# First norm of a hybrid diffusion layer: scale and shift made by blocks of channels, tokens scaled before they are transposed

## The chip, the cores and the metric

The kernel runs on one core of a Trainium2 chip, as one program. The metric is the device time of one execution in microseconds (us). Three executions of the kernel before were timed, and one more was profiled; every duration below is from that profiled one.

## The reference

One trunk layer: a modulated RMSNorm, a token mixer (latent attention beside a bidirectional mLSTM) and a mixture of 16 experts, all in float32. The change touches the first norm and what feeds it:

```python
mod_l = silu(c) @ w_mod + b_mod              # latent tokens
mod_c = silu(c_ctx) @ w_mod + b_mod          # context tokens
sh1, sc1, ... = split(mod_l, 6)              # each 1024 channels
h_l = rmsnorm(x, norm1) * (1 + sc1) + sh1    # x:   1024 tokens x 1024 channels
h_c = rmsnorm(ctx, norm1) * (1 + sc1c) + sh1c  # ctx: 256 tokens x 1024
z = h @ w_in                                 # 1024 x 4864, the input projection
```

## The kernel before

Tokens are worked in three segments of 512, 512 and 256 (the last is the context). For each segment the norm's result is wanted with channels on partitions: `hT` holds, for each of the 8 blocks `d` of 128 channels, the value rounded to fp32r (`hT[0]`) and the rest (`hT[1]`). A projection block `b` (128 of the output columns) then takes 8 x 3 matmuls: for every `d`, high weight times `hT[0]`, high weight times `hT[1]`, low weight times `hT[0]`. ScalarE makes the high weight `whi` from the loaded `wraw`, VectorE the low one `wlo`.

Scale and shift of the first norm, each 1024 channels for two kinds of token, come from two 1024 x 1024 weights, loaded in 16 tiles `wm` of 512 KB.

- Scale (`scale(k)`, L265): TensorE, with two columns of silu(c) as the stationary operand and 512 weights moving, twice per tile `k`. A tile is one block of inputs, so all eight are needed before any channel is done; the sum `mps` is copied, turned by 8 small transposes (L290) and finished in `a1`.
- Shift (`shift(k)`, L258): VectorE, one multiply with a sum along the row for each tile and each kind of token (L263). A tile is one block of outputs. The result is `b1`.
- Tokens: ScalarE squares each tile `x` (128 tokens) and sums (`jkx`, L237), VectorE makes the reciprocal root (`rstd_dve`), then four matrices `dg`, the identity times a token's factor. `turn_x` multiplies `x` by `dg`, which turns and scales in one matmul. For segment 0 the result is copied into `xT` (L279) while scale and shift are made.
- `hidden(si, d, src)` makes `hT` of one block: ScalarE `hx` = scale times value plus shift (L300), then `hT[0]` by ScalarE for odd `d` (L302) or VectorE for even `d` (L304), then VectorE the rest (L305).

`proj` (L200) is the projection, `to_xm` copies the first `N_XM` = 3 blocks' results out. All loads are issued by SyncE in one queue. The order on each engine is not the order of the code: the tile layer sets it when the program is built, and each engine then goes through its list in that order and waits at each row for what the row needs.

Of the kernel before, what the change touches and what calls it, by code (L numbers as in the profile page):

```python
# [23 lines left out]
F32 = mybir.dt.float32  # L24
F32R = mybir.dt.float32r
BF16 = mybir.dt.bfloat16
I32 = mybir.dt.int32
AF = mybir.ActivationFunctionType
ALU = mybir.AluOpType
# [4 lines left out]
P = 128  # L34
D = 1024
# [8 lines left out]
SEGS = [(0, 512), (512, 512), (1024, 256)]  # L44
# [9 lines left out]
    _o += _w  # L54
NCOL = _o
BIG = -1.0e30
N_XM = 3
U_, WK_, KEEP_, FL_, WI_ = 3, 8, 9, 10, 11

# [15 lines left out]
def body(tc, A, out, dbg=None, upto=99):  # L75
    nc = tc.nc
    dbg = dbg or {}
    V, S, G, TE = nc.vector, nc.scalar, nc.gpsimd, nc.tensor
# [5 lines left out]
    def mm(o, l, r, start, stop):  # L84
        return TE.matmul(o, l, r, start=start, stop=stop, skip_group_check=True)  # L85
# [38 lines left out]
    def col(name, j=0, w=1):  # L124
        return cols[:, COL[name] + j:COL[name] + j + w]
# [62 lines left out]
    def fetch_w(b):  # L188
        raw[b] = pw.tile([P, 8, P], F32, name="wraw", bufs=2)
        nc.sync.dma_start(raw[b], A["win"][b])  # L190

    def split_w(b):
        if b not in raw:
            fetch_w(b)
        pool, n = (px, N_XM - 2) if 2 <= b < N_XM else (pw, 2)
        hi = pool.tile([P, 8, P], F32R, name="whi", bufs=n)
        lo = pool.tile([P, 8, P], F32R, name="wlo", bufs=n)
        split(hi, lo, raw.pop(b))
        whi[b], wlo[b] = hi, lo
# [13 lines left out]
    pm = pm_.__enter__()  # L213
    ps0_ = tc.tile_pool(name="ps0", bufs=1, space=PSUM, reuse_waits="tile")
    ps0 = ps0_.__enter__()
    xT = scratch[:, 0:4, :].rearrange("p a (b n) -> p (a b) n", n=512)
    sbc = [scratch[:, 4 + c, :] for c in range(2)]
    mrow = scratch[:2, 6, :]
    xs, diag, raw, xm = {}, {}, {}, {}

    def load_x(i):
        xs[i] = (pm if i < 4 else p0).tile([P, D], F32, name=f"x{i}")
        src = A["x"][i * P:(i + 1) * P] if i < 8 else A["ctx"][(i - 8) * P:(i - 7) * P]
        nc.sync.dma_start(xs[i], src)

    def turn_x(si, d, dst):

        for c, dg in enumerate(diag[si]):
            mm(dst[:, c * P:(c + 1) * P], xs[SEGS[si][0] // P + c][:, d * P:(d + 1) * P], dg, True, True)

    def norms(si):
        o, n = SEGS[si]
        tiles = range(o // P, (o + n) // P)
        ss = p0.tile([P, len(tiles)], F32, name=f"ss{len(tiles)}", bufs=2)
        for c, i in enumerate(tiles):
            jk = p0.tile([P, D], BF16, name="jkx", bufs=1)
            S.activation(jk, xs[i], AF.Square, accum_out=ss[:, c:c + 1])  # L237
        rstd_dve(p0, ss, ss, D)
        diag[si] = []
        for c, i in enumerate(tiles):  # L240
            dg = p0.tile([P, P], F32, name="dg", bufs=5)
            V.tensor_scalar(dg, ident, ss[:, c:c + 1], None, op0=ALU.mult)
            diag[si].append(dg)

    for i in range(4):
        load_x(i)
    for c in range(2):
        for q in range(2):
            tp = ps0.tile([P, 512], F32, name="tp", bufs=2)
            for k in range(4):  # L250
                TE.transpose(tp[:, k * P:(k + 1) * P], sil[:, 4 * q + k, c:c + 1].to_broadcast([P, P]), ident)
            S.copy(sbc[c][:, q * 512:(q + 1) * 512], tp)
    norms(0)


    mps = [ps0.tile([2, 512], F32, name="mps", bufs=2) for n in range(2)]

    def shift(k):  # L258
        wt = pm.tile([P, D], F32, name="wm", bufs=9)
        nc.sync.dma_start(wt, A["wmod_s"][k * P:(k + 1) * P])  # L260
        for c in range(2):
            jk = p0.tile([P, D], BF16, name="jk", bufs=1)
            V.scalar_tensor_tensor(jk, wt, 1.0, sbc[c], op0=ALU.mult, op1=ALU.mult, accum_out=b1[:, k, c:c + 1])  # L263

    def scale(k):  # L265
        wm = pm.tile([P, D], F32, name="wm", bufs=9)
        nc.sync.dma_start(wm, A["wmod_a"][k])
        for n in range(2):
            done = mm(mps[n], sil[:, k, :], wm[:, n * 512:(n + 1) * 512], k == 0, k == 7)
        return done  # L270

    fetch_w(0)
    for k in range(8):
        done = scale(k)
        shift(k)
        with tc.issue_after(done.ins):
            tp = ps0.tile([P, 512], F32, name="tp", bufs=2)
            turn_x(0, k, tp)
        S.copy(xT[:, k, :], tp)  # L279
    split_w(0)  # L280
    for i in range(4, 8):
        load_x(i)
    fetch_w(1)
    load_x(8)
    load_x(9)
    for n in range(2):
        S.copy(mrow[:, n * 512:(n + 1) * 512], mps[n])
    mt = ps0.tile([P, 8, 2], F32, name="mps", bufs=2)
    for j in range(8):
        TE.transpose(mt[:, j, :], mrow[:, j * P:(j + 1) * P], ident[:2, :2])  # L290
    V.tensor_tensor(a1, mt, col("bmod", 8, 8)[:, :, None].to_broadcast([P, 8, 2]), op=ALU.add)
    V.scalar_tensor_tensor(a1, a1, 1.0, col("norm1", 0, 8)[:, :, None].to_broadcast([P, 8, 2]),
                           op0=ALU.add, op1=ALU.mult)
    V.tensor_tensor(b1, b1, col("bmod", 0, 8)[:, :, None].to_broadcast([P, 8, 2]), op=ALU.add)

    def hidden(si, d, src):
        n, kind = SEGS[si][1], 0 if si < 2 else 1
# [7 lines left out]
        V.tensor_sub(hT[1][si][:, d, :], hx[:, :n], hT[0][si][:, d, :])  # L305

    for d in range(8):
        hidden(0, d, xT[:, d, :])
    pm_.__exit__(None, None, None)
    hp2 = tc.tile_pool(name="hT2", bufs=1, reuse_waits="tile")  # L310
    hpool = hp2.__enter__()
# [19 lines left out]
    for si in range(3):  # L331
        if si > 0:
            norms(si)
            for d in range(8):
                tp = ps0.tile([P, 512], F32, name="tp", bufs=2)
                turn_x(si, d, tp)
                hidden(si, d, tp[:, :SEGS[si][1]])
        for b in range(N_XM):
            to_xm(b, si)
# [632 lines left out]
class Merge:  # L972
# [11 lines left out]
    def mm(self, o, l, r, start, stop):  # L984
        return self.nc.tensor.matmul(o, l, r, start=start, stop=stop, skip_group_check=True)  # L985
# [1021 lines left out]
def arrange(inp):  # L2007

    f = {k: np.asarray(v) for k, v in inp.items()}
    ca = np.ascontiguousarray  # L2010
    A = {"x": f["x"][0], "ctx": f["ctx"][0]}
    cc = np.stack([f["c"][0], f["c_ctx"]], -1)
    A["cT"] = ca(cc.reshape(8, P, 2).transpose(1, 0, 2))
    wm = f["w_mod"][0]
    A["wmod_a"] = ca(wm[:, 1024:2048]).reshape(8, P, D)
    A["wmod_s"] = ca(wm[:, :1024].T)
    A["wmod_b"] = ca(wm[:, 2048:].T)

    def bycol(v):
        return v.reshape(-1, P).T  # L2020

    cw = f["conv_w"][0].reshape(5, 8, P).transpose(2, 1, 0).reshape(P, 40)
    A["cols"] = ca(np.concatenate([bycol(f["norm1"][0]), bycol(f["norm2"][0]), bycol(f["conv_b"][0]),
                                   bycol(f["ml_norm"][0]), bycol(f["ml_skip"][0]), bycol(f["q_norm"][0]),
                                   bycol(f["kv_norm"][0]), bycol(f["b_mod"][0]), cw], 1))
    w = f["w_in"][0]
    q, kv, kr, xm, z, ga, gb = np.split(w, np.cumsum([384, 256, 64, 1024, 1024, 1024]), axis=1)
    wp = np.concatenate([xm, q, kv, kr, kr, z, ga, gb], 1)
    A["win"] = ca(wp.reshape(8, P, 38, P).transpose(2, 1, 0, 3))
    A["wgate"] = ca(f["w_gate"][0].reshape(24, P, 16).transpose(1, 0, 2))  # L2030
    A["bgate"] = f["b_gate"][0]

    def bd(n):
        b = f[n][0].reshape(8, 32, 4, 4)
        o = np.zeros((8, 32, 4, 32, 4), b.dtype)
        i = np.arange(32)
        o[:, i, :, i, :] = b.transpose(1, 0, 2, 3)
        return o.reshape(8, P, P)

    wq = f["w_uq"][0].reshape(3, P, HEADS, 192)  # L2040
    A["wuq_n"] = ca(wq[..., :128].transpose(1, 2, 0, 3))
    A["wuq_p"] = ca(wq[..., 128:].reshape(3, P, 512).transpose(1, 0, 2))
    wk = f["w_ukv"][0].reshape(2, P, HEADS, 256)
    A["wukv_k"] = ca(wk[..., :128].transpose(2, 1, 0, 3))
    A["wukv_v"] = ca(wk[..., 128:].reshape(2, P, 4, 256).transpose(2, 1, 0, 3))
    A["wout"] = f["w_out"][0]
    A["wrouter"] = ca(f["w_router"][0].reshape(8, P, NE).transpose(1, 0, 2))
    A["final_norm"] = f["final_norm"]
    gu = np.stack([f["w_e_gate"][0], f["w_e_up"][0]], 0).reshape(2, NE, 8, P, 2, 512)

    A["wgu"] = ca(gu.transpose(1, 4, 2, 3, 0, 5).reshape(NE, 2, 4, 2, P, D).transpose(0, 1, 2, 4, 3, 5))
    A["wd"] = ca(f["w_e_down"][0].reshape(NE, 4, 2, P, D).transpose(0, 1, 3, 2, 4))
    bq, bk, bv = bd("w_qblk"), bd("w_kblk"), bd("w_vblk")
    A["bdv"] = ca(bv.transpose(1, 0, 2))
    A["bdT"] = ca(np.stack([bq, bk, bv], 1).transpose(0, 3, 1, 2))
    return A
# [17 lines left out]
```

## Time and profile before

| | us |
|---|---|
| median of 3 executions | 1984.59 |
| lowest, highest | 1984.45, 1988.88 |
| profiled execution | 1984.47 |
| its span, first to last instruction | 1982.7 |
| TensorE busy | 1906.8 (96%) |
| VectorE busy | 1375.1 (69%) |
| ScalarE busy | 1049.2 (53%) |
| mean granted TensorE clock | 0.989 of full speed |

The work is pipelined, so a busy TensorE is not one at its peak. The stage that changes lies in the first 100 us of the span.

### The profile page before, as it was taken

The page shows a single profiled execution, that of the slowest core. Times are in us where ns is not written, and L with a number is a line of the kernel's source. Part 1 is how long each engine was busy: PE and PEld are TensorE (multiplying, and loading weights), DVE is VectorE, ACT ScalarE, POOL GpSimd, SP SyncE. Part 2 cuts the span into 40 slices and gives each one's busy share as a digit, 9 for nine tenths or more (in the row PEclk, how much of TensorE's full clock was granted, in tenths as well). Part 3 has the DMA queues.
Part 4 walks back from the last instruction along what each step waited for, and adds up shares of the span by engine and source line. Part 5 has one row for each costly group of instructions (what it writes and reads, how often), then busy time and mean ns, then how long its engine had stood idle before and what let it go on. Part 6 is the DMA issues. An engine that isn't in the chain of part 4 may idle for free.

```text
span 1982.7 us, 28319 instructions
## 1 busy us (share of the span) xinstructions
PE 1906.8 (96%) x10450; PEld 1604.9 (81%) x10450; DVE 1375.1 (69%) x2495; ACT 1049.2 (53%) x1609; POOL 539.6 (27%) x491
## 2 busy tenths in 40 slices
PE   7999999999999999899999999997999999999996
PEld 3898888888877887788999999785788888887773
DVE  6463555111368688777676767667899999989886
ACT  5554422122336785533443434433778788786783
POOL 0000000000025003156453545101735446354310
PEclk9999999999999999999999999998999999999998
DMA  7153376323169151212311111446899999999995
GB/s 310 51 153 90 111 241 233 96 69 116 34 209 329 46 213 38 72 62 73 103 52 46 52 45 51 172 149 253 316 366 379 384 392 379 380 393 376 375 340 212
DMA packets 160332, 384.78 MB, mean 194 GB/s; under 512 B 10161, under 2 KB 98817, under 8 KB 142529
## 3 DMA queue, kind: packets, MB, share of 16 engines
q1 hardware_dynamic: 145136, 328.68, 46.3%
q0 software_dynamic: 12752, 45.90, 7.4%
q10 hardware_dynamic: 2304, 8.39, 1.1%
q8 instruction: 82, 1.34, 0.3%
q14 instruction: 58, 0.47, 0.1%
HBM read 326.00 MB, written 56.93 MB: 193 GB/s over the span
## 4 chain that ended last, share of the span: by engine, by line
PE 82%; DVE 9%; DMA 3%; ACT 3%; issue 2%; SPq 0%; POOLq 0%; POOL 0%; DVEq 0%; ACTq 0%
PE mm L85 24%; PE s L1454 11%; PE pa L1181 8%; PE pu L1181 8%; PE py L1181 7%; PE mm L985 4%; PE pv L1454 4%; PE ab L1735 3%; PE c L1735 2%; PE tr L85 2%; DVE tl L1622 2%; PE tp L85 1%; DVE lo L881 1%; PE mps L85 1%; ACT hi L866 1%
## 5 line engine op out<-in xcount | busy, mean ns | idle before, releaser
L85 PE MATMUL mm<-hT,whi 128*128 128x512 f32 (+1 forms) x1392 | 414.8, 381 | 2.6 <-DVE hT L304 2.3
L85 PEld LDWEIGHTS mm<-hT,whi 128*128 128x128 f32 x1392 | 255.0, 189 | 52.1 <-DVE hT L304 2.4
L85 PE MATMUL mm<-hT,wlo 128*128 128x512 f32 (+1 forms) x696 | 263.0, 378 | 0.3 <-DVE wlo L89 0.3
L1254 POOL TENSOR_SCALAR g<-iota,slot 128x128 bf16<-128x128 f32 x120 | 182.6, 1537 | 229.0 <-PE tr L1284 229.0
L881 DVE TENSOR_TENSOR lo<-raw_l,hi 128x2048 fp32r<-128x2048 f32 x98 | 223.0, 2300 | 20.7 <-ACT hi L866 15.9
L866 ACT CAST hi<-raw_l 128x2048 fp32r<-128x2048 f32 x98 | 186.6, 1916 | 26.3 <-PE pu L1181 17.0
L1181 PE MATMUL py<-hi,hd 128*128 128x512 f32 x480 | 161.4, 402 | 0.0
L85 PEld LDWEIGHTS mm<-hT,wlo 128*128 128x128 f32 x696 | 131.3, 189 | 24.5 <-DVE wlo L89 0.7
L89 DVE TENSOR_TENSOR wlo<-wraw,whi 128x1024 fp32r<-128x1024 f32 x38 | 46.5, 1224 | 141.9 <-ACT whi L88 141.9
L881 DVE TENSOR_TENSOR lo<-xca,hi 128x2048 fp32r<-128x2048 f32 x58 | 132.1, 2296 | 11.4 <-ACT hi L866 6.0
L1613 POOL TENSOR_TENSOR es<-es,e 128x512 f32<-128x512 f32 x96 | 124.9, 1301 | 7.0
L1607 ACT ACTIVATE e<-s 128x512 f32<-128x512 f32 x160 | 94.5, 612 | 52.2 <-PE s L1454 52.2
L866 ACT CAST hi<-xca 128x2048 fp32r<-128x2048 f32 x58 | 110.3, 1910 | 20.6 <-PE pu L1181 19.7
L1613 POOL TENSOR_TENSOR es<-e 128x512 f32<-128x512 f32 x32 | 41.7, 1304 | 260.8 <-ACT e L1607 260.8
L88 ACT CAST whi<-wraw 128x1024 fp32r<-128x1024 f32 x38 | 40.0, 1052 | 128.4 <-PE mm L85 120.0
L1554 DVE TENSOR_TENSOR mx<-mx,s 128x512 f32<-128x512 f32 x128 | 87.9, 687 | 27.1 <-PE s L1454 24.5
L1181 PE MATMUL pa<-lo,xh 128*128 128x512 f32 x256 | 102.0, 398 | 2.4 <-DVE lo L881 2.2
L1181 PEld LDWEIGHTS py<-hi,hd 128*128 128x128 f32 x480 | 89.6, 188 | 18.1 <-DVE hd L1289 0.2
L1181 PE MATMUL pa<-hi,xh 128*128 128x512 f32 x256 | 100.8, 394 | 0.3 <-ACT xh L1310 0.3
L1181 PE MATMUL pu<-hi,xl 128*128 128x512 f32 x256 | 100.3, 392 | 0.0
L1181 PE MATMUL pu<-lo,xh 128*128 128x512 f32 x256 | 99.9, 390 | 0.0
L1181 PE MATMUL pa<-hi,xl 128*128 128x512 f32 x256 | 99.8, 390 | 0.0
(498 smaller groups left out, 4790.5 us busy)
## 6 DMA issues: line engine op xcount, KB each, us to landing
raw_l<-in_wgu SPq DMA_DIRECT2D x64, 1024.0 KB
xca<-in_wgu SPq DMA_DIRECT2D x41, 1024.0 KB
raw_l<-in_wd SPq DMA_DIRECT2D x36, 1024.0 KB
ha<-in_wgu SPq DMA_DIRECT2D x22, 1024.0 KB
wraw<-in_win SPq DMA_DIRECT2D x38, 512.0 KB
xca<-in_wd SPq DMA_DIRECT2D x19, 1024.0 KB
wt<-in_wmod_b SPq DMA_DIRECT2D x32, 512.0 KB
vk_d<-vk SPq DMA_DIRECT2D x16, 640.0 KB
```

The lines of the kernel that those rows point to most:

```text
L85: return TE.matmul(o, l, r, start=start, stop=stop, skip_group_check=True)
L89: V.tensor_sub(lo, raw, hi)
L866: self.nc.scalar.copy(h, w)
L881: self.nc.vector.tensor_sub(l, w, h)
L985: return self.nc.tensor.matmul(o, l, r, start=start, stop=stop, skip_group_check=True)
L1181: return TE.matmul(o, l, r, start=start, stop=stop, skip_group_check=True)
L1254: G.tensor_scalar(oh[:, o, :], iota, slot[:, o, e:e + 1], None, op0=ALU.is_equal)
L1454: return TE.matmul(o, l, r, start=start, stop=stop, skip_group_check=True)
L1554: V.tensor_max(new if p > 1 else new.rearrange("p (a b) -> p a b", a=2), old, ps if p > 1 else ps.rearrange("p (a b) -> p a b", a=2))
L1607: S.activation(E[p], ps, AF.Exp)
L1613: G.tensor_add(s, E[0] if p == 1 else s, E[p])
L1735: self.tc.nc.tensor.matmul(o, l, r, start=start, stop=stop, skip_group_check=True)
```

## The change

Scale and shift are made by blocks of 128 output channels. The weight of the scale is laid out by output blocks, and TensorE takes 8 matmuls per block, with the 128 x 128 weight as the stationary operand and two columns of silu(c) moving; the result needs no transpose. The shift of the first `N_SH` = 7 blocks stays on VectorE, that of the eighth goes to TensorE in the same way. Per block `d` then come scale, shift, transposes of `x` and `hidden`, in one loop. `norms` scales the tokens `x` themselves (ScalarE for segment 0, VectorE for segments 1 and 2), and `turn_x` is a plain transpose. The copies into `xT` and `mrow` are gone; `hidden` reads `tp`, of which there are three buffers and not two. The first shift tile is loaded ahead of `x`, the first projection weight after four more tiles, the second ahead of the last scale tile.

```diff
+N_SH = 7
 def turn_x(si, d, dst):
-        for c, dg in enumerate(diag[si]):
-            mm(dst[:, c * P:(c + 1) * P], xs[SEGS[si][0] // P + c][:, d * P:(d + 1) * P], dg, True, True)
+        o, n = SEGS[si]
+        for c in range(n // P):
+            TE.transpose(dst[:, c * P:(c + 1) * P], xs[o // P + c][:, d * P:(d + 1) * P], ident)
 def norms(si):
...
         rstd_dve(p0, ss, ss, D)
-        diag[si] = []
         for c, i in enumerate(tiles):
-            dg = p0.tile([P, P], F32, name="dg", bufs=5)
-            V.tensor_scalar(dg, ident, ss[:, c:c + 1], None, op0=ALU.mult)
-            diag[si].append(dg)
+            if si == 0:
+                S.activation(xs[i], xs[i], AF.Copy, scale=ss[:, c:c + 1])
+            else:
+                V.tensor_scalar(xs[i], xs[i], ss[:, c:c + 1], None, op0=ALU.mult)
+    def fetch(src):
+        t = pm.tile([P, D], F32, name="wm", bufs=9)
+        nc.sync.dma_start(t, src)
+        return t
+    ws, wa = [fetch(A["wmod_s"][:P])], []
     for i in range(4):
         load_x(i)
...
-    def shift(k):
-        wt = pm.tile([P, D], F32, name="wm", bufs=9)
-        nc.sync.dma_start(wt, A["wmod_s"][k * P:(k + 1) * P])
-        for c in range(2):
-            jk = p0.tile([P, D], BF16, name="jk", bufs=1)
-            V.scalar_tensor_tensor(jk, wt, 1.0, sbc[c], op0=ALU.mult, op1=ALU.mult, accum_out=b1[:, k, c:c + 1])
-    def scale(k):
-        wm = pm.tile([P, D], F32, name="wm", bufs=9)
-        nc.sync.dma_start(wm, A["wmod_a"][k])
-        for n in range(2):
-            done = mm(mps[n], sil[:, k, :], wm[:, n * 512:(n + 1) * 512], k == 0, k == 7)
-        return done
-    fetch_w(0)
-    for k in range(8):
-        done = scale(k)
-        shift(k)
-        with tc.issue_after(done.ins):
-            tp = ps0.tile([P, 512], F32, name="tp", bufs=2)
-            turn_x(0, k, tp)
-        S.copy(xT[:, k, :], tp)
-    split_w(0)
...
+    def matvec(dst, w):
+        w = w.rearrange("p (a b) -> p a b", b=P)
+        for k in range(8):
+            mm(dst, w[:, k, :], sil[:, k, :], k == 0, k == 7)
+    def modulation(d):
+        matvec(mt[:, 0, d, :], wa[d])
+        V.tensor_scalar(a1[:, d, :], mt[:, 0, d, :], bm1[:, d:d + 1], col("norm1", d), op0=ALU.add, op1=ALU.mult)
+        if d < N_SH:
+            for c in range(2):
+                jk = p0.tile([P, D], BF16, name="jk", bufs=1)
+                V.scalar_tensor_tensor(jk, ws[d], 1.0, sbc[c], op0=ALU.mult, op1=ALU.mult, accum_out=b1[:, d, c:c + 1])
+            src = b1[:, d, :]
+        else:
+            matvec(mt[:, 1, d, :], ws[d])
+            src = mt[:, 1, d, :]
+        V.tensor_scalar(b1[:, d, :], src, col("bmod", d), None, op0=ALU.add)
...
     for d in range(8):
-        hidden(0, d, xT[:, d, :])
+        wa.append(fetch(A["wmod_a"][d]))
+        if d < 7:
+            ws.append(fetch(A["wmod_s"][(d + 1) * P:(d + 2) * P] if d + 1 < N_SH else A["wmod_a"][8 + d + 1 - N_SH]))
+        if d == 0:
+            norms(0)
+        if d in (1, 6):
+            fetch_w(d // 6)
+        modulation(d)
+        tp = ps0.tile([P, 512], F32, name="tp", bufs=3)
+        turn_x(0, d, tp)
+        hidden(0, d, tp)
+        if d == 1:
+            split_w(0)
+    for i in range(4, 10):
+        load_x(i)
```

VectorE in segment 0, from the factors `ss` of the tokens on (`jk,b` is the shift, `a` the scale, `hT_0_101` and `hT_0_102` the two parts of `hT`). Before:

```order
L242 TENSOR_SCALAR dg<-ident,ss_150 128x128 x4
L263 SCALAR_TENSOR_TENSOR jk,b_89<-wm,xca 128x1024 x16
L291 TENSOR_TENSOR a_88<-mps,cols 128x16
L294 TENSOR_TENSOR b_89<-b_89,cols 128x16
L292 SCALAR_TENSOR_TENSOR a_88<-a_88,cols 128x16
L304 CAST hT_0_101<-hx 128x512
L305 TENSOR_TENSOR hT_0_102<-hx,hT_0_101 128x512 x2
```

And of the change, from the third shift on:

```order
L277 SCALAR_TENSOR_TENSOR jk,b_89<-wm,xca 128x1024 x2
L292 CAST hT_0_101<-hx 128x512
L282 TENSOR_SCALAR b_89<-b_89,cols 128x2
L293 TENSOR_TENSOR hT_0_102<-hx,hT_0_101 128x512 x2
L273 TENSOR_SCALAR a_88<-mps,bm_153,cols 128x2
L90 TENSOR_TENSOR wlo<-wraw,whi 128x1024
L292 CAST hT_0_101<-hx 128x512
L277 SCALAR_TENSOR_TENSOR jk,b_89<-wm,xca 128x1024
L293 TENSOR_TENSOR hT_0_102<-hx,hT_0_101 128x512
L273 TENSOR_SCALAR a_88<-mps,bm_153,cols 128x2
L277 SCALAR_TENSOR_TENSOR jk,b_89<-wm,xca 128x1024
```

The shifts, which stood in one run of 16, now stand between the making of `hT`, the low weight and, per block, a row that reads TensorE's `mps`.

TensorE at the same place (`mps` is the scale, `tp` the turned tokens, `mm` the projection). Before, two of the eight rounds:

```order
L85 MATMUL mps<-wm,sil 2x512 x2
L85 MATMUL tp<-dg,x_118 128x128
L85 MATMUL tp<-dg,x_120 128x128
L85 MATMUL tp<-dg,x_122 128x128
L85 MATMUL tp<-dg,x_124 128x128
L85 MATMUL mps<-wm,sil 2x512 x2
```

And of the change, from the third scale to the fourth:

```order
L86 MATMUL mps<-sil,wm 128x2 x8
L229 MATMUL tp<-ident,x_120 128x128
...
L229 MATMUL tp<-ident,x_126 128x128
L86 MATMUL mm<-hT_0_101,whi 128x512
L86 MATMUL mm<-hT_0_102,whi 128x512
...
L86 MATMUL mm<-hT_0_101,wlo 128x512
L86 MATMUL mm<-hT_0_101,whi 128x512
L86 MATMUL mm<-hT_0_102,whi 128x512
L86 MATMUL mm<-hT_0_101,wlo 128x512
L86 MATMUL mps<-sil,wm 128x2 x8
```

The scale of a block now stands behind matmuls of the projection, which wait for `hT` of earlier blocks and for `wlo`.

ScalarE where segment 0 ends (`jkx` squares the tokens of segments 1 and 2, `xm` copies a finished projection, the third `whi` is that of projection block 2). Before:

```order
L300 ACTIVATE hx<-xca,b_89,a_88 128x512
L88 CAST whi<-wraw 128x1024
L237 ACTIVATE jkx,ss_488<-x_319 128x1024
L329 COPY xm<-mm 128x512
L88 CAST whi<-wraw 128x1024
L237 ACTIVATE jkx,ss_488<-x_321 128x1024
L237 ACTIVATE jkx,ss_488<-x_323 128x1024
```

And of the change:

```order
L290 ACTIVATE hT_0_101<-tp,b_89,a_88 128x512
L238 ACTIVATE jkx,ss_531<-x_410 128x1024
L238 ACTIVATE jkx,ss_531<-x_412 128x1024
L331 COPY xm<-mm 128x512
L238 ACTIVATE jkx,ss_531<-x_414 128x1024
L331 COPY xm<-mm 128x512
L238 ACTIVATE jkx,ss_708<-x_416 128x1024
L238 ACTIVATE jkx,ss_708<-x_418 128x1024
L89 CAST whi<-wraw 128x1024
```

The weight of projection block 2 moved behind all the squares of segments 1 and 2.

## Rows read from the trace of the kernel before

**Rows 1.** The page: shares of the span by engine along the chain that ended last.

```profile
PE 82%; DVE 9%; DMA 3%; ACT 3%; issue 2%; SPq 0%; POOLq 0%; POOL 0%; DVEq 0%; ACTq 0%
```

**Rows 2.** Chain of waits, first 130 us: start us, us, what was waited for.

```profile
4.61 7.87 DMA wm<-in_wmod_a
...
12.53 3.57 PE mps L85 x4
...
17.93 1.81 PE mps L85 x4
19.75 1.09 PE tp L85 x8
...
39.88 1.41 ACT hx L300 x2
...
49.32 1.24 DVE wlo L89
...
50.60 10.92 PE mm L85 x46
...
92.39 6.93 PE mm L85 x56
```

**Rows 3.** Windows, all engines: busy us (instructions), granted clock, DMA share, GB/s.

```profile
20.00:40.00 20.00, 18.80 (x88) 8.55 (x86) 16.82 (x31) 6.42 (x12) 0.37 (x9) 1.00 1.03 409
...
40.00:50.00 10.00, 8.62 (x26) 5.48 (x26) 7.92 (x13) 10.00 (x14) 0.00 (x0) 0.83 0.12 46
```

**Rows 4.** Timeline: ScalarE's first square, TensorE's first transposes.

```profile
6.15 1.06 ACT L237 ACTIVATE jkx<-x 128x1024 bf16<-128x1024 f32 x1 [3.58 <-DMA x<-in_x]
...
3.69 1.97 PE L251 MATMUL tp<-ident,sil 128*128 128x128 f32 x8 [3.69 <-DVE sil L128]
```

**Rows 5.** Groups by line and shape, 0 to 130 us: busy us, mean ns, idle before.

```profile
L263 DVE SCALAR_TENSOR_TENSOR jk<-wm,xca 128x1024 bf16<-128x1024 f32 x16 | 19.6, 1225 | 0.5
L305 DVE TENSOR_TENSOR hT<-hx,hT 128x512 fp32r<-128x512 f32 x16 | 11.1, 692 | 4.3 <-ACT hT L302 3.2 <-ACT hx L300 0.8
L304 DVE CAST hT<-hx 128x512 fp32r<-128x512 f32 x8 | 3.4, 426 | 5.3 <-ACT hx L300 5.2
L89 DVE TENSOR_TENSOR wlo<-wraw,whi 128x1024 fp32r<-128x1024 f32 x5 | 6.1, 1224 | 3.0 <-ACT whi L88 3.0
L300 ACT ACTIVATE hx<-tp,b,a 128x512 f32<-128x512 f32 x8 | 6.2, 777 | 2.2 <-PE tp L85 1.6 <-DVE hT L304 0.6
L88 ACT CAST whi<-wraw 128x1024 fp32r<-128x1024 f32 x5 | 5.2, 1046 | 0.9 <-PE mm L85 0.9
```

**Rows 6.** Timeline, TensorE at 522 us: sums over partitions, one moving column.

```profile
522.78 1.84 PE L85 MATMUL tr<-ones,sqs 128*128 128x1 f32 x16
```

**Rows 7.** One line, L421, plain transposes: durations in ns, first and last start.

```profile
L421 PE MATMUL tr<-ident,sil x8: 272/272/322, 248.0 to 249.1; 128*128 128x128 f32 x8
```

**Rows 8.** One line, L1138, ScalarE scaling tokens by a factor per partition.

```profile
L1138 ACT ACTIVATE x<-x,rs x4: 1148/1150/1152, 1278.8 to 1366.6; 128x1024 f32<-128x1024 f32 x4
```

**Rows 9.** Timeline, segment 1's norm: squares on ScalarE, then VectorE.

```profile
54.02 1.06 ACT L237 ACTIVATE jkx<-x 128x1024 bf16<-128x1024 f32 x1
...
55.20 1.06 ACT L237 ACTIVATE jkx<-x 128x1024 bf16<-128x1024 f32 x1
...
54.02 0.17 DVE L162 TENSOR_SCALAR rv<-ss 128x4 f32<-128x4 f32 x1 [1.01 <-ACT jkx L237]
...
56.21 0.88 DVE L242 TENSOR_SCALAR dg<-ident,ss 128x128 f32<-128x128 f32 x4
```

**Rows 10.** Timeline, TensorE: segment 1's first projection matmuls, segment 2's first turn.

```profile
64.19 0.78 PE L85 MATMUL mm<-hT,whi 128*128 128x512 f32 x2
...
85.80 1.05 PE L85 MATMUL tp<-dg,x 128*128 128x128 f32 x8
```

**Rows 11.** Windows, TensorE alone: busy us (instructions), granted clock, DMA share, GB/s.

```profile
41.00:42.00 1.00, 0.82 (x2) 0.65 0.19 74
...
44.00:45.00 1.00, 1.00 (x4) 0.64 0.00 0
```

## Prediction before the result

> **What bounds the kernel now.** I read the page's chain first: 82% of it is TensorE [rows 1]. So what shortens the span either takes TensorE work off or closes a gap there. Then the chain of the first 130 us [rows 2], where one sees four stages. Until 12.48 the first scale tile is awaited. From 12.53 TensorE alternates scale matmuls and turned tokens, eight rounds of 1.81 + 1.09 us behind a stream of loads at 409 GB/s [rows 2, 3], which is one 512 KB tile per 1.27 us; TensorE is busy 18.80 of 20 us there, at full clock [rows 3]. From 39.88 the chain is on ScalarE (`hx`), and the window 40 to 50 says why: ScalarE is busy 10.00 of 10 us, TensorE 8.62 with nothing but early pieces of the projection to do [rows 3]. From 50.60, when the second low weight is ready, TensorE has 46 matmuls in a row (10.92 us, 0.237 each) [rows 2]. Segment 1's projection starts at 64.19, segment 2's turns at 85.80 [rows 10], and the chain stays on TensorE (56 matmuls from 92.39 to 99.32 [rows 2]). The order of every engine is the same in both programs from some 125 us on, so what is gained or lost by then is the result; I follow the time at which segment 1's projection can start.
>
> **Loads.** One shift tile ahead of `x` costs the tokens 1.27 us: the first square starts at 7.4 instead of 6.15 [rows 4], the fourth ends near 13.1 (pitch 1.18 [rows 9]). The first scale tile still lands near 12.5. The later loads lie ahead of their use: the first weight lands near 17.6, and ScalarE reaches it at 24.9; if that cover were gone, at most one tile's 1.27 us.
>
> **TensorE.** Removed are eight scale rounds, 8 x 1.81 = 14.5 us [rows 2]. Added are nine matvecs of 8 matmuls with two moving columns. No row has that shape; the nearest has one moving column, 16 records or 8 float32 matmuls in 1.84 us [rows 6], of which some 1.7 is pitch. Nine are 15.3 us. Bounds: no less than 1.5 (the weight load is the same), no more than double, 3.4, while the clock is at its low level; I take 1.6 from 30 us on and 2.4 before, where the engine has just been idle. A block's four turns cost 4 x 0.157 = 0.63 (eight start over 1.1 us [rows 7]) instead of 1.09 (four matmuls in eight records [rows 2]), and 0.98 at low clock (1.97 for eight [rows 4]). So modulation saves TensorE nothing; what is new is that `hidden` of block 0 need not wait for block 7.
>
> **ScalarE.** Removed are the copies into `xT` and `mrow`, which lay under the loads. Added are four scalings of 1.15 us [rows 8] on the way to the first turn. They wait for the factors.
>
> **VectorE, the queue that decides.** The fourth square ends at 13.1 and the factors take 2.2 us there (54.02 to 56.21 [rows 9]). But in the middle of them stands the first `a1`, which needs matvec 0: 12.5 + 2.4 + 0.2 = 15.1. The remaining six steps end at 16.5. From there the queue holds 12 shift rows x 1.225 = 14.7, 8 rests x 0.692 = 5.5, 4 roundings x 0.426 = 1.7, 2 low weights x 1.224 = 2.4 [rows 5], and some 15 small rows of 0.17 [rows 9], 2.6: 26.9 us in all, to 43.4 if it never waits. It does wait, since each `a1` row stands in line for a matvec, and that one on TensorE behind turns and projection matmuls which wait for VectorE and ScalarE in turn. Walking the two orders side by side with these durations:
> - `a1` of block 1, +2.0: its matvec stands behind three turns of token tile 0, scaled at 17.7; 17.8 + 0.7 + 2.4 = 20.9, and VectorE is there at 19.0.
> - `a1` of block 2, +1.4: its matvec stands behind the turns of block 3, which want the `tp` buffer that the first `hx` frees at 23.6; 1.0 for turns, 2.4 for the matvec: 27.0.
> - Blocks 3, 5 and 7, +0.6, +0.7, +1.0: each behind three matmuls of an earlier block that wait for its rest.
> - `b1` of block 7, +1.4: the shift that TensorE makes, a second matvec behind the first.
> - the last rest, +1.6: `hx` and `hT` of block 7 on ScalarE, 2 x 0.777 [rows 5], which cannot start before that `b1`.
>
> That is 8.7 us, and the last `hT` comes at 16.5 + 26.9 + 8.7 = 52.1. Before, it came just ahead of the `wlo` of 49.32 [rows 2]. So the projection begins sooner (near 27.6) but ends no sooner.
>
> **Segment 1's norm becomes the path.** On ScalarE its squares stand behind the last `hT` of segment 0 (51.2): three squares x 1.18 and one copy of 0.5 end near 55.2. Factors 2.2: 57.4. Four scalings on VectorE have no row of that shape. Two rows with one moving operand give the slope: 128 elements 0.22 (0.88 for 4 [rows 9]), 512 elements 0.426 [rows 5]; 1024 by the same line are 0.70. The two-operand row of 1024 is 1.225 [rows 5], the upper bound, +2.1 in sum. I take 0.68, since this row has one tensor operand as they have: 60.1. The third low weight, which stands behind it, is ready at 61.3. TensorE has finished the first two blocks near 55.0, waits, takes 12 turns, and does 22 matmuls x 0.237 = 5.2 after 61.3: 66.5. Before, that point was at 64.19 [rows 10]: **+2.3**.
>
> **Then.** Segment 1's turns cost TensorE 0.157 each and not 0.27 (1.05 to 1.09 for four [rows 2, 10]): 20 turns and 72 matmuls of 0.23, 19.7 us, take the place of 21.6 (64.19 to 85.80 [rows 10]): **-1.9**. Segment 2's 16 turns save at most 0.115 each, 1.8; ScalarE paces part of that stage, and I keep **-1.4**. The sum is 2.3 - 1.9 - 1.4 = -1.0. The profiled execution took 1984.47 (its span 1982.7 and 1.77 outside it), so 1983.5; the median of the runs shown is 0.12 above the profiled one. What a measurement can tell from no change is about 0.3%, or 5.95 us.
>
> **Rivals.**
> *Faster: VectorE does not wait.* If the matvecs run at their full-clock price from the start (1.5), and the small rows overlap, most of the 8.7 us go: the last `hT` comes at 45.0 instead of 52.1, and the whole segment-1 norm moves up with it until the last loads hold it (tokens 4 to 7 land by 35). That is 7 us earlier: 1976.5. For it: TensorE has only some 31 us of work between 12.5 and 52 at full clock. Against it: the order, in which no matvec stands ahead of work that waits. Chance 0.27.
>
> *Slower: TensorE stays at its low clock through this stage.* The trace shows the low level around waits: the granted share is 0.65 in 41 to 42 us and 0.64 in 44 to 45 [rows 11], where TensorE had waited for ScalarE [rows 2, 3], and in the first transposes of 3.69 [rows 4]. The new stream is short pieces with waits between them. At low clock 9 matvecs x 2.8 (between 1.84 and 3.68) + 32 turns x 0.246 + 42 matmuls x 0.47 are 52.8 us from 12.5 on: 65.3; the other 30 matmuls and 12 turns at full clock 9.0: 74.3 instead of 64.19, then the same -3.3: 1991.3. It decides once the low level holds for more than half of 20 to 50 us. Against it: the stage before, also with short pieces, ran at full clock from 20 to 40 [rows 3]. Chance 0.17.
>
> The Trainium skill speaks for this rival: "TensorE: Matmul & The Clock Gate", section on the PE-mode transpose, says that a transpose in that mode does not count as work that raises the clock, and the change makes plain transposes of what were matmuls. The trace neither bears this out nor refutes it: the first transposes ran at the low level, but they are the first work of all [rows 4]. By that rule alone the time would be this rival's.
>
> *Two-operand price for the scalings.* With 1.225 each: +2.1, 1985.6, within 0.3%. Chance 0.11.
>
> *Nothing changes:* the first blocks' projection moves under the wait, and everything behind the same VectorE queue ends when it did, 1984.5. Against it: VectorE's queue is new in half its rows. Chance 0.15.
>
> The forecast itself has 0.30, and by its own bounds (matvecs 1.5 to 3.4, scalings 0.68 to 1.225) lies between 1979 and 1987. **How the numbers follow.** Forecast, price of the scalings and nothing changed are all within 0.3%: 0.56. Faster 0.27, slower 0.17. To leave out no more than 2 in 10, the range takes in most of both other cases: 1975.5 to 1991.5.
>
> **What would show it.** In the changed profile: VectorE's waits for `mps` at the `a1` rows, 1 to 2 us each (right), or none (the faster rival). The last rest of segment 0 at 52 (forecast), 45 (faster), beyond 58 (slower). Granted clock of 20 to 50 us: near 1, or near 0.5 (slower rival). A TensorE gap of 2 to 3 us ahead of segment 1's turns, ended by VectorE's scaling. Scalings of 0.68 or 1.2 us. Segment 1's first projection matmul at 66.5, segment 2's first turn 19.7 us later. The forecast is wrong above all if the matvec's price is: each 0.3 us of it moves every `a1`.

## The result and the profile after

The changed kernel takes 2000.51 us (median of 4 runs, 1999.4 to 2003.33) against 1984.97 of the kernel before in the same comparison: ratio 1.0076, interval 1.0064 to 1.0087. That is slower by 15.5 us, outside the range that was given. The profiled execution took 1999.6 us of span, 16.9 more than before.

The first view is the windows of all engines in the stage that changed (columns as in [rows 3]):

```profile
20.00:30.00 10.00, 9.56 (x45) 9.16 (x46) 4.69 (x14) 4.98 (x6) 0.00 (x0) 0.50 0.90 342
30.00:40.00 10.00, 10.00 (x41) 8.99 (x39) 5.88 (x11) 1.61 (x3) 0.00 (x0) 0.50 0.47 148
40.00:50.00 10.00, 9.26 (x39) 8.47 (x40) 5.21 (x13) 1.39 (x2) 0.00 (x0) 0.50 0.93 377
50.00:60.00 10.00, 8.52 (x34) 7.44 (x33) 5.62 (x12) 4.20 (x6) 0.00 (x0) 0.50 0.15 40
```

TensorE is as busy as before, 10.00 of 10 us in 30 to 40, but its granted clock is 0.50, the lower of its two levels (1.2 GHz), where it was 1.00 over 20 to 40 us in [rows 3]. VectorE, which was to be the queue that decides, works little more than half of the time. The chain of waits says what stands in the way:

```profile
12.68 3.59 PE mps L86 x16
...
26.55 3.21 PE mps L86 x16
29.76 0.96 PE tp L229 x4
30.71 0.85 PE mm L86 x2
...
38.82 3.22 PE mps L86 x16
...
42.06 0.28 DVE a L273
...
62.89 3.21 PE mps L86 x16
66.10 5.62 PE mm L86 x17
...
75.59 0.76 DVE x L244
76.35 0.14 issue
76.49 2.16 PE tp L229 x9
...
88.45 15.75 PE mm L86 x68
```

A matvec (`mps`) costs 3.2 us all through the stage, four turns 0.96, a projection matmul 0.43. The last matvec ends at 66.1. The groups by line, VectorE from 12 to 66 us (columns as in [rows 5]), show who waits for that:

```profile
L277 DVE SCALAR_TENSOR_TENSOR jk<-wm,xca 128x1024 bf16<-128x1024 f32 x12 | 14.6, 1218 | 0.1
...
L273 DVE TENSOR_SCALAR a<-mps,bm,cols 128x2 f32<-128x2 f32 x8 | 2.2, 278 | 22.2 <-PE mps L86 22.2
```

The eight `a1` rows wait 22.2 us for `mps`, 2.2 of them ahead of the first; the shifts wait for nothing. The last rest of segment 0 ends at 68.6 (timeline of VectorE):

```profile
67.93 0.69 DVE L293 TENSOR_TENSOR hT<-hx,hT 128x512 fp32r<-128x512 f32 x1 [1.57 <-ACT hT L290]
```

The clock comes back only within the row of 17 projection matmuls that starts at 66.1 (windows of TensorE alone, columns as in [rows 11]):

```profile
68.00:69.00 1.00, 1.00 (x4) 0.50 0.00 0
69.00:70.00 1.00, 1.00 (x5) 0.81 0.00 0
```

Behind it TensorE waits for the scaled tokens of segment 1, and the matmuls after that wait are at the low price again. Segment 2's first turn, at 85.80 in [rows 10], comes last in this timeline:

```profile
76.49 2.16 PE L229 MATMUL tp<-ident,x 128*128 128x128 f32 x9 [2.97 <-DVE x L244]
78.29 1.20 PE L86 MATMUL mm<-hT,whi 128*128 128x512 f32 x2
...
104.02 0.82 PE L229 MATMUL tp<-ident,x 128*128 128x128 f32 x6
```

It is 18.2 us late. The transposes of [rows 7], which started at 248.0, are the mark that I use below for what is gained or lost by then (the same line, its number moved by two):

```profile
L423 PE MATMUL tr<-ident,sil x8: 272/273/323, 264.4 to 265.5; 128*128 128x128 f32 x8
```

They are 16.4 us late, so nearly the whole difference arises in the first 104 us.

### The profile page after: what moved, and what is told of

It reads as the page before. It is cut to its first block, busy times and chain, and to the rows that moved or that the text cites. A ratio compares the mean times of both kernels' runs of the same rounds, so it can differ in the third digit from the quotient of the medians.

```text
span 1999.6 us, 28359 instructions
## 1 busy us (share of the span) xinstructions
PE 1919.8 (96%) x10474; PEld 1633.1 (82%) x10474; DVE 1376.3 (69%) x2501; ACT 1047.7 (52%) x1603; POOL 552.0 (28%) x491
## 3 DMA queue, kind: packets, MB, share of 16 engines
q1 hardware_dynamic: 145136, 328.68, 45.9%
## 4 chain that ended last, share of the span: by engine, by line
PE 81%; DVE 9%; DMA 5%; ACT 3%; issue 2%; SPq 0%; POOLq 0%; POOL 0%; DVEq 0%; ACTq 0%
PE mm L86 25%; PE s L1456 11%; PE pa L1183 7%; PE pu L1183 7%; PE py L1183 6%; PE pv L1456 4%; PE mm L987 4%; PE ab L1737 3%; PE c L1737 2%; PE tr L86 2%; DVE tl L1624 2%; PE mps L86 1%; DVE lo L883 1%; ACT hi L868 1%; PE mm L1737 1%
## 5 line engine op out<-in xcount | busy, mean ns | idle before, releaser
L86 PE MATMUL mm<-hT,whi 128*128 128x512 f32 (+1 forms) x1392 | 419.9, 385 | 2.2 <-DVE hT L293 2.2
L1183 PE MATMUL pu<-hi,xh 128*128 128x512 f32 x256 | 99.9, 390 | 0.0
```

## The experiments

The theory after the result (A): the matvecs with two moving columns leave TensorE at its low clock, and everything that waits for them is late. The rivals: B, the plain transposes do it; C, it is only the cold start after the wait for the first scale tile; D, it is not the clock but the order of the rows. Each run has a kernel-before time beside it on the same chip (1986.51 to 1986.88 us), and the ratios go by that.

**e1, turns undone.** Four matrices `dg` and full matmuls again, everything else as changed:

```diff
-            TE.transpose(dst[:, c * P:(c + 1) * P], xs[o // P + c][:, d * P:(d + 1) * P], ident)
+            mm(dst[:, c * P:(c + 1) * P], xs[o // P + c][:, d * P:(d + 1) * P], diag[si][c], True, True)
...
```

> The change with its turns undone: four matrices dg (identity times the token's factor) and a full matmul per turn, as before; everything else as changed. Theory A (the matvecs with two moving columns hold TensorE's clock at the low level): granted clock stays near 0.5 from 12 to 65 us, a matvec 3.2 us as now, time 1997 to 2004. Rival B (the plain transposes hold it down, the Trainium skill's rule in TensorE: Matmul & The Clock Gate): clock near 1.0 from 25 us on, a matvec 1.6 to 1.8, time 1981 to 1988. Rival C (the cold start alone): as A.

2000.85 us, ratio 1.0077 (1.0060 to 1.0094): the time of A, but not A's clock. Timeline of TensorE:

```profile
28.45 1.85 PE L86 MATMUL mps<-sil,wm 128*128 128x2 f32 x16
...
43.14 1.84 PE L86 MATMUL mps<-sil,wm 128*128 128x2 f32 x16
47.05 0.79 PE L86 MATMUL mm<-hT,whi 128*128 128x512 f32 x1 [2.07 <-ACT hT L290]
...
50.36 3.41 PE L86 MATMUL mps<-sil,wm 128*128 128x2 f32 x16
```

The clock rose within a row of 30 `dg` records (23.65 to 28.4): the matvec before them cost 3.41, those after them 1.84. After a wait of 2.07 us for ScalarE it was low again, and the last two matvecs cost 3.41. So what the turns are made of matters too, which A alone had not said, and neither A nor B is all of it. The time hides a gain: the last matvec ends at 58.5 and not at 66.1. Of these 7.6 us, 5.0 are left at segment 2's first turn (99.05) and 3.4 at the mark (261.0): in segment 1 a turn by `dg` takes some 0.2 us of TensorE (30 records, two to a matmul, from 79.17 to 82.44), a transpose of the change 0.1 (12 from 84.93 to 86.16). Those 3.4 us are less than single executions of e1 differ (1999.81 to 2004.28).

**e2, 128 moving columns.** The two columns of silu(c) repeated 64 times; weight loads and sums are the same, and the sums lie in wider places of their tile:

```diff
-            mm(dst, w[:, k, :], sil[:, k, :], k == 0, k == 7)
+            mm(dst, w[:, k, :], sil[:, k, :][:, None, :].to_broadcast([P, 64, 2]), k == 0, k == 7)
...
```

> The change with the two columns of silu(c) repeated 64 times, so that a matvec's matmul moves 128 columns and not 2; weight loads and sums are the same, only the first two result columns are read. Theory A: granted clock rises to 1.0 within the first blocks, a matvec costs 1.8 to 2.3 us (eight matmuls at the price of the old turns, 0.27 each), last hT of segment 0 near 52, time 1981 to 1989. Rival B (transposes) and C (cold start): clock stays 0.5, a matvec 3.6 to 4.4, time 2000 to 2010.

1976.5 us, ratio 0.9948 (0.9931 to 0.9965): 24 us below the change and 10 below the kernel before. Timeline of TensorE, and VectorE by line:

```profile
22.12 1.95 PE L86 MATMUL mps<-sil,wm 128*128 128x128 f32 x16
23.91 0.60 PE L229 MATMUL tp<-ident,x 128*128 128x128 f32 x4
```

```profile
L273 DVE TENSOR_SCALAR a<-mps,bm,cols 128x2 f32<-128x2 f32 x8 | 2.2, 274 | 0.9 <-PE mps L86 0.9
```

With plain transposes left in place the prices are those of the full level from 17 us on: a matvec costs 1.95 (64 times the columns, and less time than the 3.2 of the change), and `a1` waits 0.9 us instead of 22.2. B falls as the cause by itself. But with this shape the tile layer had also put the rows in another order, so D is not out.

**e3, a warm start.** Three extra matmuls of 512 columns before the first matvec:

```diff
...
+    for k in range(3):
+        mm(tp, ident, sbc[0][:, :512], True, True)
```

> The change with three extra matmuls of 512 columns (their result is not used) between the first transposes and the first matvec, where TensorE waits for the first scale tile. They show a clock that has risen before the matvecs begin. Rival C (only the cold start is to blame, and a risen clock stays): clock 1.0 on through 20 to 60 us, matvecs 1.6 to 1.8, time 1980 to 1988. Theories A and B: the clock falls back to 0.5 in or after the first matvecs, time 1998 to 2004.

1999.57 us, ratio 1.0069 (1.0052 to 1.0086). Timeline of TensorE:

```profile
12.93 1.95 PE L86 MATMUL mps<-sil,wm 128*128 128x2 f32 x16 [1.57 <-DMA wm<-in_wmod_a]
17.49 0.90 PE L229 MATMUL tp<-ident,x 128*128 128x128 f32 x3 [2.61 <-ACT x L242]
18.18 3.41 PE L86 MATMUL mps<-sil,wm 128*128 128x2 f32 x16
```

The first matvec ran at the full clock, and after the next wait (2.61 us, for the scaled tokens) the level was low again. C falls. Two later matvecs, at 32.55 and 35.30, ran in part at the full level (2.12 and 2.27 us); the other six cost 3.41.

**e4, the turns alone.** The kernel before with scaled tokens and plain transposes, scale rounds as they were:

```diff
-            mm(dst[:, c * P:(c + 1) * P], xs[SEGS[si][0] // P + c][:, d * P:(d + 1) * P], dg, True, True)
...
+            TE.transpose(dst[:, c * P:(c + 1) * P], xs[o // P + c][:, d * P:(d + 1) * P], ident)
...
```

> The kernel before with one part of the change alone: tokens scaled (ScalarE for segment 0, VectorE for 1 and 2), turns as plain transposes; scale rounds with 512 moving columns, shifts and loads as before. Theory A: granted clock 1.0 in 20 to 36 us as before, scale rounds 1.81, turns 0.65 per block, time within 0.3% of the kernel before (1979 to 1990). Rival B: the clock falls to 0.5 there, scale rounds 3.6 each, time 1993 to 2002.

1980.49 us, ratio 0.9970 (0.9960 to 0.9981). Timeline and window of TensorE:

```profile
26.33 1.88 PE L85 MATMUL mps<-wm,sil 128*2 128x512 f32 x4
28.14 0.66 PE L230 MATMUL tp<-ident,x 128*128 128x128 f32 x4
```

```profile
20.00:30.00 10.00, 10.00 (x34) 1.00 1.03 410
```

Transposes between scale rounds of 512 moving columns leave the clock at 1.00, and this part of the change is worth 6 us by itself: four turns take 0.59 us of TensorE (from 28.14 to the next round at 28.73) instead of 1.09 [rows 2].

**e5, 32 moving columns,** in nearly the order of the change (silu(c) repeated 16 times):

```diff
-            mm(dst, w[:, k, :], sil[:, k, :], k == 0, k == 7)
+            mm(dst, w[:, k, :], sil[:, k, :][:, None, :].to_broadcast([P, 16, 2]), k == 0, k == 7)
...
```

> The change with 32 moving columns per matvec matmul (silu(c) repeated 16 times) instead of 2; VectorE's and ScalarE's orders are those of the change but for 12 lines of difference on VectorE and none on ScalarE. It parts the clock from the order, which also differed in the run with 128 columns. Theory A, graded by columns: the clock is at 1.0 for a part of 15 to 65 us and the time lies between 1976 and 1995; if the clock rises early with this order, time 1976 to 1984 and the order is not the cause. Rival D (the order of VectorE and TensorE, not the clock, cost the time): 1990 or more, even where the clock is at 1.0. If the clock stays at 0.5 and the time at 1998 to 2003, 32 columns do too little and the order stays open.

1998.18 us, ratio 1.0058 (1.0041 to 1.0075): the outcome in which the order stays open. Timeline of TensorE, and a window:

```profile
25.36 3.46 PE L86 MATMUL mps<-sil,wm 128*128 128x32 f32 x16
...
35.75 1.87 PE L86 MATMUL mps<-sil,wm 128*128 128x32 f32 x16
...
40.63 3.45 PE L86 MATMUL mps<-sil,wm 128*128 128x32 f32 x16
```

```profile
20.00:25.00 5.00, 4.56 (x22) 1.00 1.03 410
```

Seven of the nine matvecs are at the low price. The window's clock of 1.00 doesn't fit them; of this below.

**e10, the order held and the columns changed.** To part D from A, 128 columns, with the rows of three engines tied to the order that the change has, until segment 0 is done (`pe`, `dve` and `act` are lists of its rows, `at` the instructions; the ties set the order and add no wait):

```diff
...
+    for seq in (pe, dve, act):
+        for u, v in zip(seq, seq[1:]):
+            tc.add_manual_dep(at[v].ins, at[u].ins.name,
+                              mybir.DependencyInfo(mybir.DependencyClass.NoSync, mybir.DependencyReason.DATA), reason="order")
```

> 128 moving columns per matvec, but the rows of TensorE, VectorE and ScalarE tied to the very order that the change has, until segment 0 is done (edges between neighbouring instructions, no waits of their own). Only the matvec's moving columns differ from the change. Clock alone (theory A, order as forecast): clock 1.0 from some 25 us on, matvec 1.95, VectorE waits for mps as in the working of the prediction, last hT of segment 0 at 50 to 55, time 1980 to 1987. If the order costs nothing: 1975 to 1978, as in the run with 128 columns. Rival D (the order, not the clock): 1994 or more.

1987.36 us, ratio 1.0004 (0.9995 to 1.0014). Timeline of TensorE, VectorE by line, and its timeline:

```profile
19.52 3.62 PE L86 MATMUL mps<-sil,wm 128*128 128x128 f32 x16
...
26.00 1.95 PE L86 MATMUL mps<-sil,wm 128*128 128x128 f32 x16
...
59.65 1.73 PE L232 MATMUL tp<-ident,x 128*128 128x128 f32 x7 [2.81 <-DVE x L247]
```

```profile
L276 DVE TENSOR_SCALAR a<-mps,bm,cols 128x2 f32<-128x2 f32 x8 | 2.2, 279 | 9.6 <-PE mps L86 9.6
```

```profile
52.84 0.69 DVE L296 TENSOR_TENSOR hT<-hx,hT 128x512 fp32r<-128x512 f32 x1 [1.58 <-ACT hT L293]
...
58.75 2.74 DVE L247 TENSOR_SCALAR x<-x,ss 128x1024 f32<-128x1024 f32 x4
```

The first two matvecs are at the low price here too (3.79 and 3.62), the other seven at 1.95. Up to the end of segment 0 only the moving columns differ from the change, and the place of the sums that they need; 13 us come back. This is the kernel that the prediction described: the last `hT` at 53.5 (52.1 forecast), no change against the kernel before.

**e12, the other corner:** two columns, tied in the same way to the order of e2, with the sums in the places of e2 (against e10, beside the three lists):

```diff
...
-            at[key, k] = mm(dst, w[:, k, :], sil[:, k, :][:, None, :].to_broadcast([P, 64, 2]), k == 0, k == 7)
+            at[key, k] = mm(dst, w[:, k, :], sil[:, k, :], k == 0, k == 7)
...
```

> The other corner: 2 moving columns per matvec as in the change, but the rows of TensorE, VectorE and ScalarE tied to the order that the program with 128 columns has, until segment 0 is done. So two kinds of matvec stand in two orders each. If clock and order act apart, and the order is worth the 11 us that it is worth with 128 columns (1987.4 against 1976.5): clock near 0.5, matvec 3.2 us, time 1987 to 1992. If the order is worth little at the low clock, where the matvecs themselves pace the stage: 1995 to 2001. If the clock rises in this order with 2 columns (a theory by which the order made the clock): 1976 to 1980.

1990.51 us (1988.46 to 1995.8), ratio 1.0026 (1.0013 to 1.0038). Windows and timeline of TensorE:

```profile
30.00:40.00 10.00, 10.00 (x70) 0.88 0.85 329
40.00:50.00 10.00, 10.00 (x41) 0.50 0.58 209
```

```profile
33.35 1.84 PE L86 MATMUL mps<-sil,wm 128*128 128x2 f32 x16
...
36.21 2.18 PE L86 MATMUL mps<-sil,wm 128*128 128x2 f32 x16
38.25 1.09 PE L232 MATMUL tp<-ident,x 128*128 128x128 f32 x4
...
40.43 3.41 PE L86 MATMUL mps<-sil,wm 128*128 128x2 f32 x16
```

Here the clock had risen by 31 us and fell within the matvec of 36.21, while TensorE was busy 10.00 of 10 us: no wait came before that fall. The place of the sums is that of e2, so it is not what lowers the clock. The four corners:

| us (median) | order of the change | order of e2 |
|---|---|---|
| 2 moving columns | 2000.5 | 1990.5 |
| 128 moving columns | 1987.4 | 1976.5 |

The columns are worth 13 and 14 us, the order 10 and 11: both count. By the ratios, which set each run against the kernel before on its chip, it is 0.72 and 0.78% for the columns, 0.50 and 0.56% for the order. That the two simply add up is not shown so finely: at the mark, in the profiled executions (264.4, 249.5, 249.3 and 238.5, in the table's order), the columns are worth 15 and 11 us, the order 15 and 11.

**e8, the matvecs nearly taken out** (seven of each eight matmuls are left out):

```diff
-        for k in range(8):
-            mm(dst, w[:, k, :], sil[:, k, :], k == 0, k == 7)
+        for k in range(1):
+            mm(dst, w[:, k, :], sil[:, k, :], True, True)
```

> The change with one of the eight matmuls of each matvec; seven are left out, so scale and the eighth shift are wrong, and all else is as changed. It shows what transposes and projection alone do to the clock. Theory A: clock at 1.0 for most of 25 to 50 us, time 1970 to 1980. Rival B (transposes hold it down): clock 0.5 until the long run of projection matmuls, turns 0.23 each there, time 1982 to 1990.

1977.68 us, ratio 0.9961 (0.9947 to 0.9976): the time of A, with the clock of B in a part of the stage. Timeline of TensorE:

```profile
29.92 1.11 PE L229 MATMUL tp<-ident,x 128*128 128x128 f32 x4 [2.42 <-ACT hT L290]
```

After such waits the turns are at the low price here too (four take 0.77 us, from 29.92 to 30.69). It costs little when the matvecs, which VectorE waits for, are nearly gone: the `a1` rows wait 1.4 us in all. That fits a low clock which hurts through the matvec; but the run takes out the matvecs' work along with their low price, and so doesn't part the two.

**Versions to beat both.** e6 makes two blocks' shifts on TensorE, with 128 columns:

```diff
-N_SH = 7
+N_SH = 6
...
```

> The 128-column matvecs with the shifts of two blocks on TensorE instead of one (N_SH 6): 2.5 us less on VectorE, which was busy 9.93 of 10 us in 30 to 40 us, and 1.95 us more on TensorE. If VectorE paces segment 0 there: 1 to 3 us below the run with 128 columns (1976.5), so 1973 to 1976. If TensorE's matvecs pace it: equal or up to 2 us above, 1976 to 1979.

e7 makes the scale in two halves `h` of 512 channels in the shape of the kernel before, and all shifts on VectorE:

```diff
...
-            mm(dst, w[:, k, :], sil[:, k, :], k == 0, k == 7)
+            mm(mp, sil[:, k, :], wa[4 * h + k // 2][:, k % 2 * 512:(k % 2 + 1) * 512], k == 0, k == 7)
...
```

> Scale in two halves of 512 channels, in the shape of the kernel before (two columns of silu(c) stationary, 512 weights moving, then copied and turned); shifts all on VectorE by blocks, transposes and hidden by blocks as in the change. Theory A: no matvec with few moving columns, so the clock is at 1.0 from some 16 us on; scale 14.5 us of TensorE in all as before; the first blocks wait for four scale tiles, hx of block 0 near 26, time 1974 to 1982. Rival B (transposes): clock 0.5, 1995 or more.

e11 writes matvec and shift of the next block (`step`) ahead of the turns of this one, with 128 columns:

```diff
...
-    for d in range(8):
+    def step(d):
...
+    step(0)
+    for d in range(8):
+        if d < 7:
+            step(d + 1)
```

> 128 moving columns, and the loads, matvec and shift of block d+1 written ahead of the turns and hidden of block d, so that the scheduler takes them first. If a1 rows that wait for matvecs still pace segment 0 in the run with 128 columns: 1972 to 1976. If VectorE's own work does (it was busy 9.93 of 10 us there): 1975.5 to 1978.

e6: 1976.83 us, ratio 0.9950 (0.9933 to 0.9967). e7: 1975.22 us, 0.9942 (0.9926 to 0.9959). e11: 1976.53 us, 0.9944 (0.9928 to 0.9961). All three and e2 beat both kernels by 0.5 to 0.6%, and these runs don't tell them apart. Moving 2.5 us of shifts off VectorE brought nothing, nor did earlier matvecs: with `a1` waiting 0.9 us in all in e2, and 0.0 in e11, there was no more to take there.

## Why the prediction was wrong, step by step

**The step that failed** is the price of a matvec from 30 us on. The prediction had both bounds, 1.5 and 3.4, and took 1.6; what it set against the low clock was that "the stage before, also with short pieces, ran at full clock from 20 to 40". It read 3.21. That clock belonged to scale rounds of 512 moving columns; I took the granted clock of a stretch for something that a busy TensorE has, and carried it to other operations. All other prices of TensorE rose with it (four turns 0.96 and not 0.63, a projection matmul 0.43 and not 0.237). With it went the wait of VectorE's `a1` rows: behind the first of them 19.9 us, where 5.7 were forecast, and the last `hT` came at 68.6 instead of 52.1.

The range failed with it. The prediction said that its own bounds, with a matvec of up to 3.4, lie between 1979 and 1987, and also that each 0.3 us of the matvec moves every `a1`. The two don't go together: with 3.4 for 1.6 in six matvecs and for 2.4 in three, one behind the other, the last `hT` moves by 13.8 us (an estimate from its own terms), to some 66, and the time to some 1997.

**At the forecast clock most of the rest holds.** e10 has the change's order, and the full clock from 25 us to the end of segment 0. Its `a1` rows wait at the very blocks that the forecast named: 3.2, 0.3, 1.1, 1.0 and 1.5 us at blocks 1, 2, 3, 5 and 7 (2.0, 1.4, 0.6, 0.7 and 1.0 forecast), the last `b1` 1.6 (1.4) and the last rest 1.6 (1.6). The other figures: last `hT` 53.5 (52.1), scalings of segment 1 2.74 for four, 0.685 each (0.68; the two-operand price of 1.225 is refuted), 1987.4 against 1986.8 of the kernel before (a change of -1.0 was forecast, +0.5 measured within its interval). One thing the forecast lacked shows here as well: after the forecast wait ahead of segment 1's turns (2.81 us) the granted clock is 0.50 from 60 to 65 us, and the third projection block ends at 69.8 where 66.5 was forecast. In the changed kernel itself these steps were right: the first scale tile at 12.64 (12.5); four scalings on ScalarE back to back, and the first turn right behind the first of them (18.87); the TensorE gap ahead of segment 1's turns of 2.97 us, ended by VectorE's scaling (2 to 3). The first matvec was undersized, 3.59 for 2.4, which put the factors at 17.6 instead of 16.5. The scale rounds that went were 16.2 us and not 14.5, as the first of them had cost 3.57 [rows 2]; no other term hung on that. Behind segment 1, 18.2 us late became 16.4: the forecast gain of 1.4 in segment 2 came, as 1.8.

**The slower rival was the right mechanism, mis-sized.** It had chance 0.17 and 1991.3. It took 2.8 us for a matvec (3.2 to 3.6 measured) and left out TensorE's own waits between 12.7 and 66 us (2.61, 0.44, 0.74 and 1.48). It let the clock return after 42 projection matmuls, near 65 us; it returned after some 31, past 69, so that more of them were still to do. It also left out that after the 2.97 us wait before segment 1's turns the level is low once more, as the matmuls from 78.3 show. By its sum the third projection block was done at 74.3; it was at 84.9.

**The faster rival** (VectorE does not wait, 1976.5) is what e2 does, at 1976.5 with 0.9 us of waits at the `a1` rows and the last `hT` at 45.9 (45.0). It needed both the clock and another order; the rival named only the clock.

**The rule on transposes.** e4 and e2 have plain transposes in stretches at clock 1.00, so they don't hold it down by themselves; in e1 turns as full matmuls stood where the clock rose, and it stayed up until the wait of 45 to 47 us. The Trainium skill ("TensorE: Matmul & The Clock Gate", section on the PE-mode transpose) says only that transposes don't count as work for the clock. By that rule alone this case is not decided: e1 agrees with it in part, and in e2, e4 and the change the same transposes run at either level, with other matmuls between them.

What stays open: what the chip counts as activity. The runs show which streams ended at which level, not why.

## What to carry to other kernels

A granted clock read from a stretch holds for the operations of that stretch; when a change swaps the operations, price it at both levels and let the range reach to the slow one. If a TensorE stage looks fully busy and each of its rows costs twice its known price, look at the clock; here, repeating columns whose result nobody reads made the stage faster. And when a program is ordered by a scheduler, a change of shape changes the order too: hold the order fixed before giving a cause to the shape.

## What the runs showed of the hardware that was not expected

- 64 times the moving columns at almost no price: a matvec of 8 float32 matmuls took 1.84 us with 2 columns (e1) and 1.95 with 128 (e2) at the full level, 3.41 (the change) and 3.62 (e10) at the low one.
- The level fell within a stream in which TensorE had no wait at all (e12, within the matvec of 36.21, busy 10.00 of 10 from 30 to 40 us; in e3 likewise within that of 35.30), and had stood at the full one in e5 and e12 for some 6 to 8 us within similar streams. A TensorE that the profile shows busy throughout did not keep the level there.
- The granted clock of the windows can be wrong early in the program: e5 reads 1.00 for 20 to 25 us, while its matvecs there cost 3.46, and the kernel before reads 1.00 for 12 to 16 us, while its first scale round there cost 3.57, the later ones 1.81 [rows 2]. Up to the first change of level that is recorded, the durations decide.
